# Regrouping the small f32 products of a two-block transformer kernel on one Trainium2 core

## The chip, the cores and the metric

The kernel runs on one core of one Trainium2 chip. The metric is the device time of one execution in microseconds (us), from which the median of the runs is taken. On the chip, TensorE does matrix products in program order; its instructions appear under PE (the product) and PEld (the load of its stationary operand). VectorE (DVE), ScalarE (ACT) and GpSimd (POOL) do the rest, and SyncE (SP) and POOL issue transfers.

## The reference

Two blocks of two layers each over 256 tokens of width 1024, all in f32. The first block's even layer mixes tokens with differential attention and with HGRN2, its odd layer with dilated attention; each layer has a squared-relu FFN. The second block carries 256 latents and 256 context tokens; each layer mixes with gated linear attention (4 heads of 64), neighbourhood attention and sliding-window attention, and has a SwiGLU. Where the change lies, this is computed:

```python
def hgrn2(hq, hf, hi, hg, lb, out_g):            # 4 heads, keys and values of 128, chunks of 64
    ...
    a = jnp.einsum('nbhtk,nbhsk->nbhts', qc * jnp.exp(b - b_mid), kc * jnp.exp(b_mid - b))
    a = jnp.where(jnp.tril(jnp.ones((C, C), bool)), a, 0.0)
    o_intra = jnp.einsum('nbhts,nbhsv->nbhtv', a, vc)
    ...
    def step(state, xs):
        qo, ks, vv, dc = xs
        o_inter = jnp.einsum('bhtk,bhkv->bhtv', qo, state)
        state = dc[..., None] * state + jnp.einsum('bhsk,bhsv->bhkv', ks, vv)
        return state, o_inter

def gla_chunked(q, k, v, log_a, s0):             # 4 heads of 64, chunks of 64, both directions
    ...
    a_intra = jnp.where(lower, jnp.einsum('bhncd,bhnsd->bhncs', q_in, k_in), 0.0)
    o_intra = jnp.einsum('bhncs,bhnse->bhnce', a_intra, vc)
    chunk_state = jnp.einsum('bhnsd,bhnse->bhnde', k_end, vc)
    ...
    o_inter = jnp.einsum('bhncd,nbhde->bhnce', q_in, s_enter)
    o = (o_intra + o_inter).reshape(B, H, T, dv).astype(v.dtype)
    return o, s_final
```

## The kernel before

A token tile is 128 tokens, so each stream has two (t = 0, 1), and a token tile holds two chunks of 64 (c = 0, 1). Weights stream from HBM and are split into a high and a low part (`wh`, `wl`; L214 on ScalarE, L216 on VectorE); a projection is three products each (L279 to L281 in the first block and in projections in general, L325 to L327, L826 to L828 and L851 to L853 in the FFN, L1465 to L1467, L1544 to L1546 and L1570 to L1572 in the second block's SwiGLU). Products of attention and of the recurrences are plain f32; transposes (L177) go through TensorE too.

The program is a list of items (a projection's block, a step of attention, a row of the modulation), woven by hand. Their instructions are then put in order on each engine by a scheduler that simulates times, so a change in one item can move others. PSUM has eight banks under four tags: `acc` 4, `sc` 2, `sm` 1, `fil` 1. A product that needs a bank waits until the earlier tile of that tag has been read.

The places that matter:
- `hg2` (L620 to L637): HGRN2's output of a token tile. For each chunk and head an intra-chunk product of 64x64 (L620, `aT` holds the masked scores, zero between the chunks), for chunks after the first also one with the state (L622); then per chunk the four state products (L627), which VectorE turns into the next state (L630, L633). ScalarE copies the result (L637). The out-projection (L279) follows.
- `sums` in `gla` (L1091): for each chunk four products of 64 rows give the chunk's state sums, copied by VectorE into `gcs` (L1094, L1095).
- `scores` in `gla` (L1113): for each chunk four products of 64 rows give the scores, masked by VectorE (L1116).
- `outputs` in `gla` (L1154): for each chunk and head two intra-chunk products (one per direction; contraction over 128 tokens, 64 of them zero, 64 output rows), then up to two with the states entering the chunk.
- `one` in `attention` (L1220): for each of a pair's two heads, the scores against its own keys and, in the latents, against the context's.

The modulation (L955) multiplies weights that POOL loads into two buffers (`fr`, L953); its items are woven among the others. In `gla` and `attention` the class `Stream` chooses PSUM tags: the latents (`ctx` false) use `acc` and `sc`, the context `fil` and `sm`.

Of the kernel before, what the change touches and what calls it, by code (L numbers as in the profile page):

```python
# [14 lines left out]
ALU = mybir.AluOpType  # L15
AX = mybir.AxisListType

P = 128
# [10 lines left out]
def unit_plan():  # L29
    """[k block, k blocks, columns, their number] of the pieces in which each weight is loaded."""  # L30
# [89 lines left out]
def body(ctx: ExitStack, tc: tile.TileContext, A: dict, out: bass.AP):  # L120
# [62 lines left out]
    def params():  # L183
        """feature-major gains of the second block and conditioning vectors."""
# [51 lines left out]
    def weave(a, b, ahead=False):  # L236
        """items of b spread evenly between those of a."""
# [72 lines left out]
    def projT(w, kdim, c0, nb, xs, evac, tag="acc"):  # L310
        """items of a projection to feature-major: nb blocks of 128 columns, two to a tile of evac(tiles)."""
# [24 lines left out]
    class Rot:  # L336
        """PSUM tiles from several tags in turn."""
# [10 lines left out]
    def urgent(fn, offset=URG):  # L348
        """fn, whose instructions go ahead of others that are ready."""
        def f(*args):  # L350
            with tc.high_priority(offset=offset):
                return fn(*args)
        return f

    def split_evac(hi, lo, ps):
        """psum -> hi/lo f32r."""
        S.copy(hi, ps)
        V.tensor_tensor(lo, ps, hi, ALU.subtract)

    def to_xT(src, xT, t, ps_of, g=None, b=None):  # L360
        """token-major [128, 1024] -> feature-major hi/lo, optional per-feature scale/shift."""
# [26 lines left out]
    def ln_half(t, ci, st):  # L388
        """statistics of one finished half of token tile t."""
# [4 lines left out]
    def layer_norm(t, st, l, n, xT):  # L394
        """token tile t normalised with gain and shift in place, and its transpose."""
# [18 lines left out]
    def rms_rstd(ms, tag, eps=1e-6):  # L414
        """1 / rms from the mean squares of the halves."""
# [3 lines left out]
    def head_rms(ps, nh, hd, eps, tag):  # L419
        """psum [P, nh, hd] -> rstd [P, nh]."""  # L420
# [7 lines left out]
    def masked(ps3, d):  # L428
        """select the in-chunk causal positions of [P, 4, P] scores; zero elsewhere."""
# [5 lines left out]
    # ---------------------------------------------------------------------- block 1  # L435

    class XT:
        """a transposed array: high and low parts of its token tiles, and of both tiles side by side."""
# [19 lines left out]
    def rope1(tl, t, nh):  # L458
        """partial rope in place on token-major tl [P, nh, 64]."""
# [11 lines left out]
    def qkT_evac(ps, dst, t, scale, n):  # L471
        """rope and transpose n columns of q or k; dst [P, n / 128, 256]."""
# [10 lines left out]
    def softmax_pair(ps, mask, nk):  # L483
        """ps: two score tiles [P, nk]; returns unnormalised p [P, 2, nk] and 1 / sums [P, 2]."""
# [12 lines left out]
    def pipeline(steps, *stages):  # L497
        """items: the first stage of step i goes with the second of step i - 1 and so on."""
# [9 lines left out]
    # -------- even mixer  # L508
    def even_mixer(xs, y, ynew):
# [4 lines left out]
        def setup():  # L514
# [16 lines left out]
            # lower bounds: softmax over the two rows, four heads on four partitions, then to all of them  # L531
# [32 lines left out]
        def hg1a(t):  # L564
            """cumulative decays of one token tile, feature-major, and to the end of the chunk."""
# [45 lines left out]
        def hg2(t):  # L611
            qo, kst, dec, aT = hgq[t]
            vv = st["vv"]
            o3 = q4(PT("acc"))
            for c in range(2):
                n = 2 * t + c
                r = slice(64 * c, 64 * c + 64)
# [1103 lines left out]
```

## Time and profile before

| | |
|---|---|
| runs | 1965.17, 1967.50, 1971.89 us; median 1967.5 us |
| profiled execution, span from first to last instruction | 1978.5 us; no other time of it was taken |
| that span against the median | 11.0 us longer |
| mean granted TensorE clock | 0.968 |
| PE busy | 1894.7 us, 96% |
| VectorE, ScalarE, GpSimd busy | 1233.7 us, 1006.1 us, 169.4 us |
| transfers | 338.89 MB, mean 171 GB/s |

The profile is of one execution. Busy shares say which engine holds the kernel on the whole; which wait ends last in a stage has to be read from that stage. An f32 product shows up as two matmul instructions, a transpose as one. "us" of a group in the timeline includes the time in which its last product runs out, so durations of a stretch are better read from start to start.

### The profile page before, as it was taken

What the parts mean: (1) busy time and instruction counts of PE and PEld (TensorE: products, weight loads), DVE (VectorE), ACT (ScalarE), POOL (GpSimd) and SP (SyncE); (2) the same over time, 40 slices, a digit from 0 to 9 for tenths busy, and PEclk for the clock granted to TensorE, in tenths of its full rate; (3) what the DMA queues carried; (4) which work ended last, traced back from release to release, by engine and by line L of the source; (5) the groups of instructions that cost most, each with busy time, mean ns of one, the idle gap of its engine ahead of it and who ended that gap; (6) DMA issues with size and microseconds to landing.
All of it is one profiled execution on the core that took longest, in us unless ns stands there. A gap on an engine that the chain in (4) does not pass through costs nothing. (4 is left out here: it accounts for less than half of the span.)

```text
span 1978.5 us, 32280 instructions
## 1 busy us (share of the span) xinstructions
PE 1894.7 (96%) x12593; PEld 1605.1 (81%) x12593; DVE 1233.7 (62%) x2325; ACT 1006.1 (51%) x1669; POOL 169.4 (9%) x230
## 2 busy tenths in 40 slices
PE   8989999997999889999999999999999999989998
PEld 6766798887688578887687988999999996669997
DVE  5563656647467466765767775577655667754455
ACT  6353555535456355554556663354546556344443
POOL 3111300003100030000300000000000000210000
PEclk9997999999899879999999999999999999989999
DMA  8753654544576545456553345555665455455663
GB/s 288 244 168 127 233 188 152 179 139 150 187 223 210 173 148 172 141 165 216 177 167 116 99 141 169 158 181 180 183 184 160 136 180 168 140 170 167 183 184 107
DMA packets 101540, 338.89 MB, mean 171 GB/s; under 512 B 12212, under 2 KB 13516, under 8 KB 101388
## 3 DMA queue, kind: packets, MB, share of 16 engines
q1 hardware_dynamic: 86124, 286.00, 46.0%
q0 software_dynamic: 15264, 50.84, 7.7%
q8 instruction: 99, 1.62, 0.3%
q14 instruction: 53, 0.43, 0.1%
HBM read 335.73 MB, written 1.05 MB: 170 GB/s over the span
## 5 line engine op out<-in xcount | busy, mean ns | idle before, releaser
L216 DVE TENSOR_TENSOR wl<-wr,wh 128x1024 fp32r<-128x1024 f32 (+3 forms) x562 | 646.3, 1153 | 408.4 <-ACT wh L214 399.2
L214 ACT CAST wh<-wr 128x1024 fp32r<-128x1024 f32 (+3 forms) x562 | 549.1, 980 | 623.8 <-PE sc L1466 123.3
L279 PE MATMUL acc<-wh,mh 128*128 128x256 f32 (+3 forms) x400 | 131.4, 336 | 2.7 <-ACT mh L378 2.0
L280 PE MATMUL acc<-wl,mh 128*128 128x256 f32 (+3 forms) x400 | 131.2, 329 | 2.4 <-DVE wl L216 2.4
L281 PE MATMUL acc<-wh,ml 128*128 128x256 f32 (+3 forms) x400 | 131.0, 330 | 0.0
L279 PE MATMUL acc<-wh,xh 128*128 128x512 f32 (+3 forms) x304 | 120.0, 401 | 4.1 <-ACT wh L214 2.2
L280 PE MATMUL acc<-wl,xh 128*128 128x512 f32 (+3 forms) x304 | 118.8, 392 | 0.2
L281 PE MATMUL acc<-wh,xl 128*128 128x512 f32 (+3 forms) x304 | 117.3, 387 | 0.1
L953 POOL DMA_DIRECT2D fr<-in_w_mod_dram x90 | 48.9, 545 | 646.8 <-PE fil L955 532.9
L851 PE MATMUL acc<-wh,a 128*128 128x512 f32 x256 | 101.4, 400 | 0.0
L852 PE MATMUL acc<-wl,a 128*128 128x512 f32 x256 | 101.0, 395 | 0.0
L853 PE MATMUL acc<-wh,a 128*128 128x512 f32 x256 | 100.9, 396 | 0.0
L1465 PE MATMUL sc<-xh,wh 128*128 128x256 f32 x352 | 100.8, 286 | 0.0
L1466 PE MATMUL sc<-xl,wh 128*128 128x256 f32 x352 | 100.2, 285 | 0.0
L1467 PE MATMUL sc<-xh,wl 128*128 128x256 f32 x352 | 100.1, 285 | 0.0
L1466 PE MATMUL sc<-ml,wh 128*128 128x256 f32 x352 | 98.9, 281 | 0.0
L1465 PE MATMUL sc<-mh,wh 128*128 128x256 f32 x352 | 98.8, 281 | 0.0
L1467 PE MATMUL sc<-mh,wl 128*128 128x256 f32 x352 | 98.7, 280 | 0.0
L955 PE MATMUL fil<-fr,cT 128*32 128x256 f32 x720 | 64.9, 427 | 25.9 <-DMA fr<-in_w_mod_dram 25.8
L279 PEld LDWEIGHTS acc<-wh,mh 128*128 128x128 f32 x400 | 75.1, 189 | 15.5 <-issue 4.8
L280 PEld LDWEIGHTS acc<-wl,mh 128*128 128x128 f32 x400 | 75.7, 189 | 9.1 <-DVE wl L216 3.1
L281 PEld LDWEIGHTS acc<-wh,ml 128*128 128x128 f32 x400 | 75.4, 189 | 7.3 <-issue 0.6
(574 smaller groups left out, 4912.6 us busy)
## 6 DMA issues: line engine op xcount, KB each, us to landing
wr<-in_ffn_w_dram SPq DMA_DIRECT2D x128, 512.0 KB, 3.5
fr<-in_w_mod_dram POOLq DMA_DIRECT2D x90, 512.0 KB, 4.8
wr<-in_w_gate_dram SPq DMA_DIRECT2D x66, 512.0 KB, 3.8
wr<-in_w_up_dram SPq DMA_DIRECT2D x66, 512.0 KB, 4.2
wr<-in_w_down_dram SPq DMA_DIRECT2D x66, 512.0 KB, 3.8
wr<-in_w_in_dram SPq DMA_DIRECT2D x40, 384.0 KB, 3.5
wr<-in_ev_w_in_dram SPq DMA_DIRECT2D x28, 512.0 KB, 5.2
wr<-in_w_in_dram SPq DMA_DIRECT2D x28, 512.0 KB, 3.5
```

The lines of the kernel that those rows point to most:

```text
L214: S.copy(hi, raw)
L216: V.tensor_tensor(lo, raw, hi, ALU.subtract)
L279: mm(o, xh[:, k, :], wh[:, kk, :], start=(u == 0 and kk == 0), stop=False)
L280: mm(o, xh[:, k, :], wl[:, kk, :], start=False, stop=False)
L281: mm(o, xl[:, k, :], wh[:, kk, :], start=False, stop=(u == nu - 1 and kk == 1))
L851: mm(o, hh[:, b, ts_], wh[:, kk, :], start=(b == 0), stop=False)
L852: mm(o, hh[:, b, ts_], wl[:, kk, :], start=False, stop=False)
L853: mm(o, hl[:, b, ts_], wh[:, kk, :], start=False, stop=(b == 3))
L955: mm(ps[32 * g:32 * g + 32, 0:256], cT[:, k, :], raw[:, 256 * g:256 * g + 256], start=(k == 0), stop=(k == KD - 1), tile_position=(0, 32 * g))
L1465: mm(o, wh[:, kk, bs], mh, start=(k == 0 and b == 0), stop=False, skip_group_check=True)
L1466: mm(o, wh[:, kk, bs], ml, start=False, stop=False, skip_group_check=True)
L1467: mm(o, wl[:, kk, bs], mh, start=False, stop=(k == 7), skip_group_check=True)
```

## The change

Five regroupings, and no other work: comments and docstrings that go with them are left out here, and line numbers shift by up to 15.
- `one`: the products of a pair's heads alternate.
- `hg2`: one 128x128 product per head gives the intra-chunk part of both chunks; then the state products of both chunks, head by head; last the products with the states.
- `sums` and `scores`: the products of the two chunks alternate, into two PSUM tiles. The new `e.pair` gives them: `fil` and `acc` in the context (`sm` and `fil` in its last layer, where it has no outputs), `acc` twice in the latents.
- `outputs`: the intra-chunk products over all 128 output rows, eight in place of sixteen, then the products with the states by direction, head and chunk.

```diff
 def hg2(t):
             o3 = q4(PT("acc"))
-            for c in range(2):
-                n = 2 * t + c
-                r = slice(64 * c, 64 * c + 64)
-                for h in range(4):
-                    hs = slice(h * P, (h + 1) * P)
-                    mm(o3[r, h, :], aT[r, h, r], vv[r, t, hs], start=True, stop=(n == 0))
-                    if n > 0:
-                        mm(o3[r, h, :], qo[:, h, r], states[n][:, h, :], start=False, stop=True)
-                if n < 3:
-                    c3 = q4(rot())
+            for h in range(4):
+                mm(o3[:, h, :], aT[:, h, :], vv[:, t, h * P:(h + 1) * P], start=(h == 0), stop=False, skip_group_check=True)
+            ns_ = [n for n in (2 * t, 2 * t + 1) if n < 3]
+            c3s = [q4(rot()) for _ in ns_]
+            for h in range(4):
+                for n, c3 in zip(ns_, c3s):
+                    r = slice(64 * (n % 2), 64 * (n % 2) + 64)
+                    mm(c3[:, h, :], kst[r, h * P:(h + 1) * P], vv[r, t, h * P:(h + 1) * P], start=True, stop=True)
...
+            for h in range(4):
+                for c in range(2):
+                    r = slice(64 * c, 64 * c + 64)
+                    if 2 * t + c:
+                        mm(o3[r, h, :], qo[:, h, r], states[2 * t + c][:, h, :], start=False, stop=(h == 3),
+                           skip_group_check=True)
...
 class Stream:
+            self.pair = (Rot("fil"), Rot("acc")) if self.ctx else (Rot("acc"), Rot("acc"))
...
 def sums(t):
-            for c in range(2):
-                r = slice(64 * c, 64 * c + 64)
-                cs = rot().rearrange("p (d h n) -> p d h n", d=2, h=2)
-                for d in range(2):
-                    for hp in range(2):
-                        mm(cs[:, d, hp, :], ke[r, d, hp * P:(hp + 1) * P], e.v[r, t, hp * P:(hp + 1) * P],
+            cs2 = [new().rearrange("p (d h n) -> p d h n", d=2, h=2) for new in (e.pair if need_out else (Rot("sm"), Rot("fil")))]
+            for d in range(2):
+                for hp in range(2):
+                    for c in range(2):
+                        r = slice(64 * c, 64 * c + 64)
+                        mm(cs2[c][:, d, hp, :], ke[r, d, hp * P:(hp + 1) * P], e.v[r, t, hp * P:(hp + 1) * P],
                            start=True, stop=True)
...
 def scores(t):
-                pa = rot().rearrange("p (d h n) -> p d h n", d=2, h=2)
-                for d in range(2):
-                    for hp in range(2):
-                        mm(pa[:, d, hp, :], en[r, d, hp, :], ep[r, d, hp, :], start=True, stop=True)
+            pa2 = [new().rearrange("p (d h n) -> p d h n", d=2, h=2) for new in e.pair]
+            for d in range(2):
+                for hp in range(2):
+                    for c in range(2):
+                        r = slice(64 * c, 64 * c + 64)
+                        mm(pa2[c][:, d, hp, :], en[r, d, hp, :], ep[r, d, hp, :], start=True, stop=True)
...
 def outputs(t):
-            for c in range(2):
-                r = slice(64 * c, 64 * c + 64)
+            for h in range(4):
+                for d in range(2):
+                    mm(op[h % 2][:, h // 2, :], aT_[t][h % 2][:, d, h // 2, :], e.v[:, t, h * 64:(h + 1) * 64],
+                       start=(h < 2 and d == 0), stop=False, skip_group_check=True)
+            for d in range(2):
                 for h in range(4):
                     hr = slice(64 * (h % 2), 64 * (h % 2) + 64)
-                    vs = e.v[:, t, h * 64:(h + 1) * 64]
-                    ops = [(aT_[t][h % 2][:, d, h // 2, r], vs) for d in range(2)]
-                    for d in range(2):
+                    for c in range(2):
+                        r = slice(64 * c, 64 * c + 64)
                         s0 = states[d, 2 * t + c]
                         if s0 is not None:
-                            ops.append((ep[hr, d, h // 2, r], s0[hr, h // 2, :]))
-                    for i, (a, b) in enumerate(ops):
-                        mm(op[h % 2][r, h // 2, :], a, b, start=(i == 0), stop=(i == len(ops) - 1))
+                            mm(op[h % 2][r, h // 2, :], ep[hr, d, h // 2, r], s0[hr, h // 2, :], start=False,
+                               stop=(d == 1 and h > 1), skip_group_check=True)
...
 def one(hp, t):
-                p = PT(e.sc[c])
-                for i, kk in enumerate(ks):
-                    mm(p[:, i * 256:(i + 1) * 256], q, kk, start=True, stop=True)
-                ps.append(p)
+                ps.append(PT(e.sc[c]))
+                qks.append([(q, kk) for kk in ks])
+            for i, pair in enumerate(zip(*qks)):
+                for p, qk in zip(ps, pair):
+                    mm(p[:, i * 256:(i + 1) * 256], *qk, start=True, stop=True)
```

The scheduler's order on PE shows what this becomes. A row is a line, an operation, its output and inputs (with buffer numbers) and the output's shape; "x4" means four alike in a row. First, `outputs` of the latents in the second block's first layer, before: `a` is the values, `t_2229` and `t_2231` the masked scores, `cf` and `gs` states.

```order
L1154 MATMUL acc_11799<-a_2090_10256,t_2229_10966 64x64 x2
L1154 MATMUL acc_11799<-cf_669_3327,t_2192_10747 64x64
L1154 MATMUL acc_11799<-gs_11633,t_2192_10747 64x64
L1154 MATMUL acc_11800<-a_2090_10256,t_2231_10974 64x64 x2
L1154 MATMUL acc_11800<-cf_669_3327,t_2192_10747 64x64
L1154 MATMUL acc_11800<-gs_11633,t_2192_10747 64x64
```

And after, the same place:

```order
L1152 MATMUL acc_11775<-a_2090_10232,t_2230_10947 128x64 x2
L1152 MATMUL acc_11776<-a_2090_10232,t_2231_10950 128x64 x2
L1152 MATMUL acc_11775<-a_2090_10232,t_2230_10947 128x64 x2
L1152 MATMUL acc_11776<-a_2090_10232,t_2231_10950 128x64 x2
L1161 MATMUL acc_11775<-cf_669_3319,t_2192_10723 64x64
L1161 MATMUL acc_11775<-gs_11594,t_2192_10723 64x64
L1161 MATMUL acc_11776<-cf_669_3319,t_2192_10723 64x64
L1161 MATMUL acc_11776<-gs_11594,t_2192_10723 64x64
```

Before, the two kinds of product take turns for 32 products; after, eight products of the one kind come first and then 16 of the other, with nothing between.

Second, the end of `hg2` up to the out-projection, before (L622 with L620 in turn goes on to the end, with L697, L177, L955 and four L627 between):

```order
L955 MATMUL fil_1179<-fr_1243,cT_72 32x256 x4
L622 MATMUL acc_1267<-t_302_1277,t_97_438 64x128
L620 MATMUL acc_1267<-a_264_1130,t_123_565 64x128
L622 MATMUL acc_1267<-t_302_1277,t_97_438 64x128
L620 MATMUL acc_1267<-a_264_1130,t_123_565 64x128
```

After, from the same modulation group on:

```order
L958 MATMUL fil_1179<-fr_1243,cT_72 32x256 x4
L177 MATMUL sm_1229<-ident_61,t_274_1162 128x128 x2
L637 MATMUL acc_1267<-t_303_1282,t_97_438 64x128 x4
L637 MATMUL acc_1325<-t_304_1284,t_136_612 64x128
L700 MATMUL acc_1350<-a_194_870,a_259_1107 128x128 x6
L958 MATMUL fil_1179<-fr_1313,cT_72 32x256 x4
L177 MATMUL sm_1233<-ident_61,t_289_1216 128x128 x2
L623 MATMUL sm_1330<-a_264_1130,t_137_613 128x128 x4
L700 MATMUL acc_1350<-a_194_870,a_259_1107 128x128 x2
L958 MATMUL fil_1179<-fr_1319,cT_72 32x256 x4
L637 MATMUL acc_1325<-t_313_1335,t_136_612 64x128
L637 MATMUL acc_1325<-t_304_1284,t_136_612 64x128
```

The products with the states (L637) stand in runs, the intra-chunk ones have left this stretch for an earlier place, and a modulation group (`fr_1443`) now stands between the last L637 and the out-projection's first L279.

Third, the context's `sums` of its first token tile among the first block's FFN, before (the second chunk's four follow 28 rows later in the same way):

```order
L826 MATMUL sc_2722<-xh_1619,wh_2643 128x256
L1091 MATMUL fil_2699<-c_430_1947,t_559_2693 128x128 x4
L827 MATMUL sc_2722<-xl_1620,wh_2643 128x256
```

After:

```order
L829 MATMUL sc_2714<-xh_1611,wh_2635 128x256
L1095 MATMUL fil_2691<-c_430_1939,t_559_2685 128x128
L1095 MATMUL acc_2692<-c_430_1939,t_559_2685 128x128
L1095 MATMUL fil_2691<-c_430_1939,t_559_2685 128x128
L1095 MATMUL acc_2692<-c_430_1939,t_559_2685 128x128
```

Both chunks' products (eight in all) now stand together and alternate between two PSUM tiles.

## Rows read from the trace of the kernel before

**Rows 1.** The page, busy us (share of the span) and instructions of each engine.
```profile
PE 1894.7 (96%) x12593; PEld 1605.1 (81%) x12593; DVE 1233.7 (62%) x2325; ACT 1006.1 (51%) x1669; POOL 169.4 (9%) x230
```
**Rows 2.** Waits of PE: line, releaser, us in total, times, longest.
```profile
PE fil L955 <- DMA fr<-in_w_mod_dram: 25.8, 17, 4.8
PE fil L177 <- DVE t L1348: 10.2, 1, 10.2
PE sc L826 <- ACT mh L378: 7.0, 1, 7.0
```
**Rows 3.** Two stretches: busy us of each engine, granted clock, DMA share, GB/s.
```profile
core 0: us, PE busy (x) PEld busy (x) DVE busy (x) ACT busy (x) POOL busy (x), PEclk, DMA share, GB/s
146.00:170.00 24.00, 23.81 (x97) 12.85 (x96) 4.06 (x14) 0.73 (x2) 1.58 (x3) 0.50 0.31 97
1690.00:1735.00 45.00, 43.09 (x428) 31.45 (x426) 29.53 (x111) 18.53 (x54) 9.58 (x16) 1.00 0.40 129
```
**Rows 4.** Timeline of PE, `outputs` of the latents: start us, us, instructions.
```profile
1200.25 0.45 PE L1154 MATMUL acc<-a,t 128*64 128x64 f32 x4
1200.63 0.33 PE L1154 MATMUL acc<-cf,t 64*64 64x64 f32 x2
1200.79 0.28 PE L1154 MATMUL acc<-gs,t 64*64 64x64 f32 x2
...
1206.23 0.39 PE L1544 MATMUL fil<-xh,wh 128*128 128x256 f32 x1
```
**Rows 5.** The same for the context's first token tile.
```profile
406.12 0.45 PE L1154 MATMUL acc<-c,t 128*64 128x64 f32 x4
...
411.63 0.39 PE L826 MATMUL sc<-xh,wh 128*128 128x256 f32 x1
```
**Rows 6.** Timeline of PE, runs of narrow full-size tiles and of 64-column tiles.
```profile
308.01 1.05 PE L1067 MATMUL fil<-cst,t 128*128 128x128 f32 x8
308.82 0.36 PE L826 MATMUL sc<-xh,wh 128*128 128x256 f32 x1
...
1113.20 0.66 PE L1277 MATMUL acc<-fr,sv 128*64 128x128 f32 x8
1113.69 0.61 PE L1277 MATMUL acc<-fr,csv 128*64 128x128 f32 x8
```
**Rows 7.** PE in the context's `sums`: groups of L1091, then the timeline around one.
```profile
L1091 PE MATMUL fil<-c,t 64*128 64x128 f32 x32 | 4.6, 285 | 0.0
...
317.31 0.28 PE L826 MATMUL sc<-xh,wh 128*128 128x256 f32 x1
317.51 1.16 PE L1091 MATMUL fil<-c,t 64*128 64x128 f32 x8
318.60 0.39 PE L827 MATMUL sc<-xl,wh 128*128 128x256 f32 x1
318.82 0.28 PE L828 MATMUL sc<-xh,wl 128*128 128x256 f32 x1
```
**Rows 8.** Timeline of PE, attention's score products of one pair of heads.
```profile
1023.01 0.71 PE L1220 MATMUL sc<-a,a 64*128 64x256 f32 x4
...
1024.08 0.39 PE L279 MATMUL acc<-wh,xh 128*128 128x256 f32 x1
```
**Rows 9.** Timeline of PE, the latents' `scores`, both chunks in a row.
```profile
1125.49 1.71 PE L1113 MATMUL acc<-t,t 64*128 64x128 f32 x16
1127.13 0.50 PE L1570 MATMUL acc<-wh,c 128*128 128x512 f32 x1
```
**Rows 10.** Timeline of PE, HGRN2: idle time before and its releaser in brackets.
```profile
144.31 0.64 PE L955 MATMUL fil<-fr,cT 128*32 128x256 f32 x8 [1.43 <-DMA fr<-in_w_mod_dram]
146.79 0.69 PE L622 MATMUL acc<-t,t 128*64 128x128 f32 x2
147.41 0.69 PE L620 MATMUL acc<-a,t 64*64 64x128 f32 x2
...
170.49 0.79 PE L279 MATMUL acc<-wh,mh 128*128 128x512 f32 x1 [0.68 <-ACT t L637]
```

More of the change, by code (lines that the diff above doesn't have):

```diff
@@ L614, in hg2 @@
             o3 = q4(PT("acc"))
-            for c in range(2):
-                n = 2 * t + c
-                r = slice(64 * c, 64 * c + 64)
-                for h in range(4):
-                    hs = slice(h * P, (h + 1) * P)
-                    mm(o3[r, h, :], aT[r, h, r], vv[r, t, hs], start=True, stop=(n == 0))
-                    if n > 0:
-                        mm(o3[r, h, :], qo[:, h, r], states[n][:, h, :], start=False, stop=True)
-                if n < 3:
-                    c3 = q4(rot())
-                    for h in range(4):
-                        hs = slice(h * P, (h + 1) * P)
-                        mm(c3[:, h, :], kst[r, hs], vv[r, t, hs], start=True, stop=True)
-                    ns = t2([P, 4, P])
-                    if n == 0:
-                        V.tensor_copy(ns, c3)
-                    else:
-                        for h in range(4):
-                            V.scalar_tensor_tensor(ns[:, h, :], states[n][:, h, :], dec[:, h, c:c + 1], c3[:, h, :],
-                                                   ALU.mult, ALU.add)
-                    states[n + 1] = ns
+            for h in range(4):
+                mm(o3[:, h, :], aT[:, h, :], vv[:, t, h * P:(h + 1) * P], start=(h == 0), stop=False, skip_group_check=True)
@@ new lines, in hg2 @@
+            ns_ = [n for n in (2 * t, 2 * t + 1) if n < 3]
[4 more added lines that the diff above has]
+                    mm(c3[:, h, :], kst[r, h * P:(h + 1) * P], vv[r, t, h * P:(h + 1) * P], start=True, stop=True)
+            for n, c3 in zip(ns_, c3s):
+                ns = t2([P, 4, P])
+                if n == 0:
+                    V.tensor_copy(ns, c3)
+                else:
+                    for h in range(4):
+                        V.scalar_tensor_tensor(ns[:, h, :], states[n][:, h, :], dec[:, h, n % 2:n % 2 + 1], c3[:, h, :],
+                                               ALU.mult, ALU.add)
+                states[n + 1] = ns
@@ L1085, in sums @@
             dec_[t] = dec
-            for c in range(2):
-                r = slice(64 * c, 64 * c + 64)
-                cs = rot().rearrange("p (d h n) -> p d h n", d=2, h=2)
-                for d in range(2):
-                    for hp in range(2):
-                        mm(cs[:, d, hp, :], ke[r, d, hp * P:(hp + 1) * P], e.v[r, t, hp * P:(hp + 1) * P],
+            cs2 = [new().rearrange("p (d h n) -> p d h n", d=2, h=2) for new in (e.pair if need_out else (Rot("sm"), Rot("fil")))]
[4 more added lines that the diff above has]
+                        mm(cs2[c][:, d, hp, :], ke[r, d, hp * P:(hp + 1) * P], e.v[r, t, hp * P:(hp + 1) * P],
                            start=True, stop=True)
+            for c, cs in enumerate(cs2):
                 cc = T([P, 2, 2, 64], F32, "gcs", 4)
@@ L1107, in scores @@
             aT_[t] = []
-            for c in range(2):
-                r = slice(64 * c, 64 * c + 64)
-                pa = rot().rearrange("p (d h n) -> p d h n", d=2, h=2)
-                for d in range(2):
-                    for hp in range(2):
-                        mm(pa[:, d, hp, :], en[r, d, hp, :], ep[r, d, hp, :], start=True, stop=True)
+            pa2 = [new().rearrange("p (d h n) -> p d h n", d=2, h=2) for new in e.pair]
[4 more added lines that the diff above has]
+                        mm(pa2[c][:, d, hp, :], en[r, d, hp, :], ep[r, d, hp, :], start=True, stop=True)
+            for pa in pa2:
                 a = t2([P, 2, 2, P])
@@ L1207, in one @@
                     nc.sync.dma_start(nbt[0], A["na_bias"][l, hp])
-            ps = []
+            ps, qks = [], []
             mx = T([P, 2, 2], F32, e.p + "mx2", 3)
```

2 lines of the change are left out of this document (removed).

## The prediction
> **What bounds the kernel now.** I read the busy shares first, then the waits of PE (TensorE's matmuls), then single stretches of PE's timeline where the changed products run. PE is busy for 96% of the span [rows 1]; all its idle time is some 84 us, of which the largest single causes are the modulation weights (25.8 us in 17 waits), one wait of 10.2 us for a normalisation and one of 7.0 us [rows 2]. So nearly everywhere a microsecond less of work on PE is a microsecond less of span, as long as the next thing in PE's queue is ready. In the HGRN2 stage this can be seen directly: between 146 and 170 us PE is busy for 23.81 of 24 us, VectorE for 4.06 and ScalarE for 0.73, and TensorE's granted clock is 0.50, the 1.2 GHz level [rows 3]. No transfer and no other engine holds PE there; it holds them.
>
> An f32 product stands in the trace as two instructions; I count these and call them records.
>
> **The linear attention's output products (`outputs`).** Before, a token tile of the latents takes 64 records, in turns of four with a 128-row, 64-column weight tile (the intra-chunk products) and four with a 64x64 tile (the products with the state). The tile at 1200 us begins at 1200.25 and the next instruction starts at 1206.23: 5.98 us, and a turn of four comes round every 0.37 us, 0.093 us a record [rows 4]. The context's first tile has 56 records (two of its states are zero): 5.51 us [rows 5]. After, the order shows 16 records of 128x128 in one run and then 32 (context: 24) of 64x64 in one run. Full-size records of narrow products cost 0.81/8 = 0.10 us at 308 us [rows 6]; I take 0.11, as the shape in front is another one: 1.8 us. The state records are not to be seen in one run before. Upper bound: the 0.093 us of today without the switch of shape that comes every four; a turn at 1200.63 with two records in 0.16 us gives 0.08 each even so [rows 4], and I put the bound at 0.06. Lower bound: neighbouring records now write different column halves, and 64-column records in that arrangement, twice as wide, come every 0.49/8 = 0.06 us [rows 6], so half of it, 0.03. That is 0.9 to 1.9 us, of which I take 0.9, since the rows at 1113 us are such alternating tiles; the two switches that are left I estimate at 0.3 us. Sum 3.0 us (to 4.0). Saved: 3.0 us in each of four latent tiles (2.0 to 3.4), 12 us; in each of the two context tiles 5.5 - (1.8 + 0.7 + 0.6) = 2.4 us (1.9 to 2.8), 4.8 us. Together **16.8 us** (12 to 19). The merged product itself saves almost nothing: 16 records at 0.11 stand for 32 at 0.06. What goes is the switching every four records.
>
> The Trainium skill speaks against the merging: "TensorEngine Tiling (Array Packing)", in its overview and in "When to Use Tiling", wants a contraction of 64 or less kept as two row tiles, for up to twice the speed, which a merged 128x128 product gives up. By it the intra-chunk part would be better off split and regrouped. The rows at 1200 us show today's 64-wide tiles coming four to 0.37 us; whether split tiles in another order would overlap, no run here shows yet, and the rule alone would take the 12 us to the lower bound of 8.
>
> **The state products of the context (`sums`).** Eight clusters of four products with one 64-row tile (in the first layer 32 records [rows 7], in the second as many) run alone. At 317 us the instruction before starts at 317.31, the cluster at 317.51 and the second instruction behind at 318.82; two plain instructions are 0.12 us each, so the cluster costs 1.51 - 0.24 = 1.27 us [rows 7], of which 8 records at 0.11 are 0.9 and the change of shape 0.4. After, both chunks alternate between two row halves and two PSUM banks, in four clusters of 16. For alternating rows the score products of attention are the nearest row: 16 records of 256 columns between 1023.01 and 1024.08, 0.067 us each [rows 8]. At 0.06 the double cluster costs 1.0 + 0.4 = 1.4 in place of 2.5. Saved 4 x 1.2 = **4.8 us** (1.6 if only the switch is saved, 5.6 at best).
>
> **The same in the latents (`sums`, `scores`).** There both chunks already run back to back, 16 records in 1125.49 to 1127.13, 1.64 us [rows 9]; alternated, 1.4 at most and 1.1 at least: 0.4 us in each of eight clusters, **3.5 us** (0 to 4.5). The context's score clusters stay split by the scheduler in the order after; I cost them at nothing.
>
> **HGRN2 (`hg2`).** In the half-clock stretch L622 and L620 take turns, 128x64 and 64x64, a pair of records every 0.62 us [rows 10]. Ten L620 pairs and all twelve L622 pairs (24 records) lie there. The order after has all intra-chunk products (L617) ahead, at full clock, where they cost 16 x 0.11 = 1.8 us against the 1.3 of the six early L620 pairs (12 records at the same 0.11); so 10 x 0.62 = 6.2 us go and 0.5 come. The L622 pairs (L637 after) come in runs of 4, 1 and 7: 24 records at 0.12 to 0.21 us of half clock plus three switches of 0.3 are 3.8 to 5.9 us in place of 12 x 0.62 = 7.4. Against that: the third state product now follows right behind a transpose into the one `sm` buffer and waits for VectorE's copy of it, some 0.7 us, as does the 0.7 us wait of L279 now [rows 10]; and one more modulation group of about 1 us is moved ahead of the out-projection. Its data are no wait: its buffer comes free some 5 us before. The out-projection should start at 163 to 164 instead of 170.49: **7 us** (3 to 10; if the clock does not fall at all, the remaining 17 us of half-clock work shrink by half and it is 15).
>
> **Attention's score products.** Whole groups (both heads, 16 records) already overlap: 1.07 us [rows 8]. The alternation as such is worth nothing. But the scheduler left 36 contiguous runs of them in the latents and now leaves 28; a run less is a switch of 0.4 us less: 3 us, of which I take **2** (0 to 3), since some gaps were beside other row products.
>
> **Sum.** 16.8 + 4.8 + 3.5 + 7 + 2 = 34 us of PE time. Not all reaches the end. Modulation weights are re-issued when PE has freed their buffer, so part of what is saved ahead of such a wait is waited out: 17 waits with a mean of 1.5 us [rows 2], of which some four lie behind the changed places; in the second latent layer (1690 to 1735 us) PE is idle for 1.9 us already and VectorE is busy for two thirds of the time [rows 3], so that there PE will wait for the masks and normalisations. I take off 5 us (0 to 12). Net -29 us: the profiled span of 1978.5 would be 1949.5. The profiled execution is 11 us above the median of the runs; the change is absolute and I carry it over: 1967.5 - 29 = **1938.5 us**. VectorE, ScalarE, GpSimd and SP keep their instructions in number; the order moves some of them, under PE's cover.
>
> **Rivals.**
> 1. The regrouping only removes switches: state records stay at 0.06 us and row halves do not overlap better than today. Then outputs 12, context sums 1.6, HGRN2 6, scores 2, less 3: 18 us, 1949 us. For it: nothing before shows 64x64 tiles in a favourable order. Against: [rows 6] and [rows 8] show both kinds of overlap. Chance 0.2. The rule above on split tiles would end here too.
> 2. Waits eat it: PE reaches each wait for weights, masks and normalisations earlier and stands there; the 12 us of the bound and half of the rest are lost, about 12 us are left, 1955 us. Against: 96% busy [rows 1]. Chance 0.12.
> 3. The clock stays high through HGRN2: another 8 to 10 us, about 1929 us and, with the upper bounds, down to 1922. For it: the low clock comes with just these small products [rows 3, 10]. Against: before 146 us PE also stood idle for 1.43 us on a weight transfer, and that stays. Chance 0.1.
> 4. Slower: the dense overlapped clusters, with the idle time behind them, bring TensorE to the 1.2 GHz level in the latents' stages, as the stage at 146 us has it. There the low level lasts 27 us, of which half is lost, 13.5 us; in four such stages it is 54 us, less the 34 saved: 1988 us. It decides if three of the four stages fall. Against: 1690 to 1735 us is full of such products and stands at 1.00 [rows 3]. Chance 0.04.
> 5. Nothing measurable: rivals 1 and 2 together, or the context's new use of the four `acc` buffers, which the FFN's down products also take, holds PE for 1 to 2 us at each of its eight clusters. The order leaves some 30 matmuls between, which is 4 us, so I expect no wait. Chance 0.04.
>
> **How the numbers follow.** The main case has 0.5 (1931 to 1946 us). A measurement of this kernel can tell about 0.3%, 6 us. Faster by more than that: the main case and rivals 1 to 3, 0.92, less a little for what no row shows: 0.89. Within 0.3%: 0.06. Slower: 0.05. The range takes in the main case, rivals 1 and 2 and most of 3: 1924 to 1957 us.
>
> **What would show it.** Output clusters of the latents at 3 us and of the context at 3.1; L1095 (now L1091) clusters of 16 records in 1.0 to 1.1 us; L279 of the out-projection near 163.5 us and the clock back at 1.00 by 167; PE's busy time down by 30 to 34 us, its waits up by under 5. I am wrong if output clusters last 4 us or more, if the waits of PE grow by over 10 us, or if new stretches at 0.50 appear.

## The result and the profile after

The changed kernel takes 1952.76 us (median of 9 runs, 1948.19 to 1961.66); the kernel before, in runs beside it, 1969.11 us (9 runs). The two medians are 16 us apart; the ratio on record is 0.9898, 95% interval 0.987 to 0.9925, which is some 20 us (15 to 26), where 29 were forecast. The time lies in the range, 14 us above the predicted 1938.5 and above the main case (1931 to 1946 us).

The profiled execution has a span of 1949.5 us, 29.0 less than the one before, which is the forecast of the profiled span to the digit. That is in part luck, as the runs of before showed later: 68 of its executions have spans of 1972.0 us in the mean, and the one that was profiled, 1978.5, lies in the upper fifth of them. The page after:

```profile
span 1949.5 us, 32053 instructions
PE 1859.0 (95%) x12481; PEld 1582.9 (81%) x12481; DVE 1230.2 (63%) x2325; ACT 1006.3 (52%) x1669; POOL 168.0 (9%) x230
```

PE is busy for 35.7 us less than before [rows 1], and idle for 90.5 us in place of 83.8. Both profiles stand at the 1.2 GHz level for about as long, 128 us before and 131 after, but not at the same places: outside HGRN2's stage it is 100 us before and 131 after. The waits of PE after, which answer to [rows 2]:

```profile
PE fil L958 <- DMA fr<-in_w_mod_dram: 30.7, 19, 7.5
PE sc L829 <- ACT mh L378: 9.3, 1, 9.3
PE fil L177 <- DVE t L1357: 8.8, 2, 7.4
```

The modulation weights are waited for 4.9 us longer, the longest wait is 7.5 us in place of 4.8, and the wait of the first block's second FFN has grown by 2.3 us.

**The output products.** Timeline of PE, the latents' `outputs` of layer 0 (L1152 the merged products, L1161 those with the states), against [rows 4]:

```profile
1176.39 1.90 PE L1152 MATMUL acc<-a,t 128*128 128x64 f32 x16
1178.21 0.27 PE L1161 MATMUL acc<-cf,t 64*64 64x64 f32 x1
1178.22 0.27 PE L1161 MATMUL acc<-gs,t 64*64 64x64 f32 x1
1178.23 0.27 PE L1161 MATMUL acc<-cf,t 64*64 64x64 f32 x1
1178.23 0.27 PE L1161 MATMUL acc<-gs,t 64*64 64x64 f32 x1
1178.32 0.22 PE L1161 MATMUL acc<-cf,t 64*64 64x64 f32 x1
...
1178.84 0.38 PE L1553 MATMUL fil<-xh,wh 128*128 128x256 f32 x1
```

2.45 us from start to start, where it was 5.98. Sixteen merged records take 1.82 us, 0.114 each. The 32 records with the states take 0.63 us, 0.02 each: four of them start within 0.02 us of each other, by the program's order one for each quarter of the array, and the next four follow 0.06 to 0.11 us after these. The three other latent tiles take 2.45, 2.55 and 3.26 us, the two context tiles 2.44 each. Before it was 5.92 to 5.97 us four times and 5.51 twice, so 19.3 us went.

**The state products.** The context's `sums` of the first tile, against [rows 7]:

```profile
303.51 0.28 PE L829 MATMUL sc<-xh,wh 128*128 128x256 f32 x1
303.72 0.37 PE L1095 MATMUL fil<-c,t 64*128 64x128 f32 x1
303.72 0.37 PE L1095 MATMUL acc<-c,t 64*128 64x128 f32 x1
303.93 0.27 PE L1095 MATMUL fil<-c,t 64*128 64x128 f32 x1
303.94 0.27 PE L1095 MATMUL acc<-c,t 64*128 64x128 f32 x1
...
304.81 0.39 PE L830 MATMUL sc<-xl,wh 128*128 128x256 f32 x1
```

Sixteen records in 1.09 us, as long as eight took before: the two row halves run as pairs, 0 to 10 ns apart.

**HGRN2.** The out-projection's first L279 starts at 153.74 us in place of 170.49 [rows 10]:

```profile
141.40 0.64 PE L958 MATMUL fil<-fr,cT 128*32 128x256 f32 x8 [1.54 <-DMA fr<-in_w_mod_dram]
144.55 1.09 PE L637 MATMUL acc<-t,t 128*64 128x128 f32 x10
151.83 1.09 PE L637 MATMUL acc<-t,t 128*64 128x128 f32 x14
153.74 0.50 PE L279 MATMUL acc<-wh,mh 128*128 128x512 f32 x1
```

Between 139 and 154 us the granted clock is 1.00. In this execution it is rival 3: the stage was not only shorter, it was not at the 1.2 GHz level at all.

### The profile page after: what moved, and what is told of

Same layout as the page of the kernel before. It is cut to its first block, busy times and chain, and to the rows that moved or that the text cites. A ratio compares the mean times of both kernels' runs of the same rounds, so it can differ in the third digit from the quotient of the medians.

```text
span 1949.5 us, 32053 instructions
## 1 busy us (share of the span) xinstructions
PE 1859.0 (95%) x12481; PEld 1582.9 (81%) x12481; DVE 1230.2 (63%) x2325; ACT 1006.3 (52%) x1669; POOL 168.0 (9%) x230
## 5 line engine op out<-in xcount | busy, mean ns | idle before, releaser
L279 PE MATMUL acc<-wh,mh 128*128 128x256 f32 (+3 forms) x400 | 131.8, 336 | 0.0
L279 PE MATMUL acc<-wh,xh 128*128 128x512 f32 (+3 forms) x304 | 119.9, 401 | 2.6 <-ACT xh L378 1.9
L1474 PE MATMUL sc<-mh,wh 128*128 128x256 f32 x352 | 98.7, 280 | 0.0
L958 PE MATMUL fil<-fr,cT 128*32 128x256 f32 x720 | 65.9, 422 | 31.2 <-DMA fr<-in_w_mod_dram 30.7
L279 PEld LDWEIGHTS acc<-wh,mh 128*128 128x128 f32 x400 | 75.2, 189 | 12.4 <-issue 4.8
L829 PE MATMUL sc<-mh,wh 128*128 128x256 f32 x256 | 74.1, 291 | 9.3 <-ACT mh L378 9.3
```

The lines of the kernel that those rows point to most:

```text
L279: mm(o, xh[:, k, :], wh[:, kk, :], start=(u == 0 and kk == 0), stop=False)
L829: mm(o, wh[:, kk, bs], mh, start=(k == 0 and b % 2 == 0), stop=False, skip_group_check=True)
L1474: mm(o, wh[:, kk, bs], mh, start=(k == 0 and b == 0), stop=False, skip_group_check=True)
```

## The experiments

Each execution comes with its span and its mean granted clock. From these I work out two numbers. The time at the 1.2 GHz level is 2 x (1 - mean clock) x span. The clock-free span is the span less half of that time; it is a measure, not a time that was run. For the 68 executions of before the first number goes from 86 to 139 us, and the span grows by 0.42 us for each of these us (correlation 0.95), so most of the scatter of this kernel goes with the clock; as 0.42 is less than a half, the measure takes off a little too much. The clock-free span scatters by 1 to 3 us only. Each kernel ran beside the kernel before, in one of several batches, and a ratio compares within the batch. The mean of before at the lower level is 110 to 115 us in the four batches that show it.

| kernel | ratio to before, 95% | mean us at the 1.2 GHz level | clock-free span, us |
|---|---|---|---|
| before, 68 executions | 1 | 113 | 1915.7 |
| before, unchanged, as a run of its own | 1.001 (0.9984 to 1.0036) | 116 | 1915.8 |
| the change, 9 and 6 runs | 0.9898 (0.987 to 0.9925), 0.989 (0.9858 to 0.9921) | 125 | 1889.4 |
| outputs alone | 0.9881 (0.985 to 0.9913) | 103 | 1897.2 |
| HGRN2 alone | 0.9956 (0.9933 to 0.9979) | 102 | 1914.3 |
| sums and scores alone | 0.9957 (0.9927 to 0.9986) | 122 | 1902.0 |
| attention's scores alone | 1.0033 (1.0002 to 1.0063) | 125 | 1917.1 |
| the change without HGRN2's part | 0.9895 (0.9857 to 0.9934) | 129 | 1888.3 |
| the change without attention's part | 0.9837 (0.9805 to 0.9869) | 107 | 1885.5 |
| the change, old product order in attention | 0.9854 (0.9815 to 0.9893) | 114 | 1884.4 |
| the change, outputs split by columns | 0.9874 (0.9844 to 0.9904) | 130 | 1883.1 |
| the same without attention's part | 0.9811 (0.9785 to 0.9837) | 110 | 1879.2 |
| outputs split, sums and scores | 0.9845 (0.9808 to 0.9883) | 120 | 1881.3 |

**1. Before once more.** The kernel is unchanged.

> The kernel before, unchanged, profiled a second time. Theory A: the granted clock of 0.50 from 146 to 173 us comes from this kernel's HGRN2 products; the second profile shows it again, with the out-projection's first L279 near 170.5 us. Theory B: which stretches fall to the lower level differs from one execution to the next; then HGRN2 may stand at 1.00 here, L279 comes near 160 us, and the span is some 10 us under 1978.5. Time: the same as before, ratio 1.000 within 0.4%.

HGRN2 fell again, but for less long: 17 us, with L279 at 166.55. Kernels further down that have the same HGRN2 code differ as much. One window of each trace, by its granted clock (the column before the last two): before again; outputs alone, whose `hg2` is the old one; the change without HGRN2's part; attention's scores alone.

```profile
143.50:161.00 17.50, 17.50 (x77) 9.68 (x71) 2.94 (x10) 0.59 (x1) 1.05 (x2) 0.51 0.28 90
```
```profile
140.00:158.00 18.00, 16.82 (x121) 10.28 (x122) 7.18 (x23) 2.64 (x10) 2.11 (x4) 1.00 0.61 212
```
```profile
144.50:175.50 31.00, 30.32 (x114) 17.74 (x113) 6.63 (x20) 6.91 (x29) 3.78 (x6) 0.50 0.27 84
```
```profile
144.00:175.00 31.00, 30.32 (x116) 17.93 (x116) 6.21 (x19) 6.16 (x25) 3.71 (x6) 0.50 0.27 84
```

In seven profiles the old `hg2` stands at the lower level for 17 to 31 us (five times), for 3 us or not at all. Theory B holds, though not in this one profile: the same code falls in one execution and not in another. In the seven profiles with the new `hg2` the stretch is 0 to 10 us long.

**2. Outputs alone.**

```diff
# before, with outputs() of the change and nothing else
+            for h in range(4):
+                for d in range(2):
+                    mm(op[h % 2][:, h // 2, :], aT_[t][h % 2][:, d, h // 2, :], ...
```

> Only the linear attention's outputs are regrouped (eight 128x128 products, then the products with the states). Theory A (terms add up): six clusters of 2.45 to 2.6 us in place of four of 5.97 and two of 5.5, 19 us less of PE time, and 14 to 19 us less of time, ratio 0.990 to 0.993. Rival (waits eat it): clusters as short, but PE waits grow by 8 us or more, ratio 0.995 to 0.998.

1950.0 us, ratio 0.9881, more than forecast and as fast as the whole change. Clock-free it is 18.5 us less, which is what went from the clusters in this profile (34.8 us before, 16.3 here); the rest is less time at the lower level. The rival falls: PE is idle for 81.3 us in place of 83.8, so nothing of it is waited out.

**3. HGRN2 alone.**

```diff
# before, with hg2() of the change and nothing else
+                mm(o3[:, h, :], aT[:, h, :], vv[:, t, h * P:(h + 1) * P], start=(h == 0), ...
```

> Only HGRN2's output is regrouped. Theory A: the regrouped products keep the 2.4 GHz level through the stage, the out-projection's L279 starts near 154 us instead of 170.5, and 10 to 13 us of the 17 stay to the end: ratio 0.9935 to 0.995. Theory B: the clock level is drawn anew in each execution and the regrouping as such is worth 6 to 8 us: ratio 0.996 to 0.997, and L279 somewhere between 154 and 164 us as the clock falls.

Ratio 0.9956, some 9 us, but clock-free only 1.4 us; the rest is the lower level (102 us in place of 113). L279 starts at 159.26 us, with 10 us at 0.50 in the stage. Theory B, in the main: clock-free the regrouped products are 2.5 us ahead at the out-projection, and 0.4 us at 271 us (times in before), so most of it is waited out behind the stage. In the mean of 12 runs the gain is there all the same (the interval lies below 1), and most of it is the lower level; in company it does not show, as experiment 6 has it.

**4. Sums and scores alone.**

```diff
# before, with e.pair, sums() and scores() of the change
+                    for c in range(2):
+                        mm(cs2[c][:, d, hp, :], ke[r, d, hp * P:(hp + 1) * P], ...
```

> Only sums and scores of the linear attention alternate their chunks between two PSUM tiles. Theory A: four clusters of 16 records of 1.09 us in the context's sums in place of eight of 1.08, and 1.1 in place of 1.5 to 1.64 in the latents: 5 + 4 = 9 us less of PE time, 6 to 9 us less of time, ratio 0.9955 to 0.997. Rival: the context's products in the acc tiles hold the FFN's accumulators up, PE waits grow by as much, ratio 0.999 to 1.002.

Ratio 0.9957, as expected; clock-free 13.7 us less, more than the 9 of the clusters, with 9 us more at the lower level against it. Of the other 5 us, 3.3 can be found: the latents' attention scores, whose code is here as before, stand in 32 contiguous runs of 35.5 us in all, where before has 37 of 38.9 us. The scheduler, with the new order in front of it, breaks up fewer of them. The last 2 us stay open. The waits for the `acc` banks that rival 5 named do not appear (PE is idle for 84.7 us in place of 83.8).

**5. Attention's score products alone.**

```diff
-                p = PT(e.sc[c])
-                for i, kk in enumerate(ks):
-                    mm(p[:, i * 256:(i + 1) * 256], q, kk, start=True, stop=True)
+            for i, pair in enumerate(zip(*qks)):
+                for p, qk in zip(ps, pair):
+                    mm(p[:, i * 256:(i + 1) * 256], *qk, start=True, stop=True)
```

> Only the score products of a pair's heads alternate. I compare the span less half of the time at the 1.2 GHz level (clock-free span), 1915.7 us before. Theory A: the alternation itself is worth nothing, but the scheduler leaves the groups whole more often, and a half group takes 1.06 us as a whole one does: clock-free span 4 to 8 us less, ratio 0.996 to 0.999 with the clock level drawn at random. Rival: it is this part that makes the sum of the parts (-33.6 us clock-free for the other three alone) larger than the whole (-27.2): clock-free span 4 to 8 us more.

Slower by 0.33%, interval just above 1. The latents' score products themselves did get shorter, summed over the timeline 36.0 us in 28 contiguous runs in place of 38.9 in 37; the clock-free span is 1.4 us longer all the same, and the time at the lower level 12 us. So neither came: not the 4 to 8 us less of theory A, and not the rival's 4 to 8 us more.

**6. The change again, and without one part.** `after_again` is the change unchanged; `no_hg2` has the old `hg2`, `no_one` the old score products; `tiles_first` takes both PSUM tiles first, as the change does, and then does the products in the old order:

```diff
-            for i, pair in enumerate(zip(*qks)):
-                for p, qk in zip(ps, pair):
+            for p, head in zip(ps, qks):
+                for i, qk in enumerate(head):
                     mm(p[:, i * 256:(i + 1) * 256], *qk, start=True, stop=True)
```

> The changed kernel, unchanged, once more beside the others. Theory A: clock-free span 1888.5 within 3 us, and some 127 us at the lower clock level, more than the 114 of before, so that the time is 18 to 22 us less: ratio 0.988 to 0.9915. Theory B: the lower level's total was drawn high in the nine runs; it comes back to 114 us and the ratio to 0.986.

> The changed kernel with HGRN2's output as before. Theory A: HGRN2's regrouping is worth 1.4 us clock-free, as alone: clock-free span 1889 to 1892, the time within 5 us of the changed kernel's. Theory B: HGRN2's regrouping sets the order downstream and costs there what the parts lose against their sum: clock-free span 1882 to 1886 and the time 4 us or more below the changed kernel's.

> The changed kernel with attention's score products as before (one head after the other). Theory A: alternating them makes PE wait for the second bank and moves waits to places where the clock then falls (as at 1599 us); without it the clock-free span is 1 to 3 us under the changed kernel's 1889.4, the time at the lower level is some 10 us shorter, and the time 4 to 8 us less: ratio 0.9855 to 0.9875. Rival: the alternation saves in the combination what it does not save alone; clock-free span 2 us or more above, ratio 0.990 or more.

> The changed kernel, with both PSUM tiles of a pair taken before the score products as in the change, but the products in the old order, one head after the other. Theory A (the alternating order of the products is what costs): PE's order is then that of the kernel without the regrouping of attention, so ratio 0.982 to 0.9855, some 107 us at the lower level and no wait of 7 us at the modulation weights. Rival (taking both tiles early is what costs): as the changed kernel, ratio 0.988 to 0.991.

The change repeats: 0.989, 122 us at the lower level, so that level was not drawn high in the first nine runs. Without HGRN2's part it is the same kernel in time (0.9895), so its 9 us alone are not found again in company. Without attention's part it is at 0.9837, faster than forecast and 10 to 12 us faster than the change; in `tiles_first` it is at 0.9854. PE's order is the same in these two kernels, instruction by instruction, and clock-free they are 4 and 5 us below the change: the alternating order of the products is what costs, not the early banks. In time alone the interval of `tiles_first` still touches the change's. Of the 10 to 12 us, 4 are clock-free; half of the 18 us less at the lower level would be 9, but some 4 of the 18 can belong to the batches, which were not the same.

Where the 4 are lost is seen on the way through the program. The table gives how far each kernel is ahead of before, clock-free, at the same projection products of both traces (profiled executions; the left column is the time in before). Two profiles of one kernel differ by 1 to 4 us in it, as the two columns of the change show.

| at us | outputs alone | sums, scores alone | attention alone | the change | the change again | without attention | split, without attention |
|---|---|---|---|---|---|---|---|
| 271 | -1.0 | -0.9 | -0.2 | 1.9 | 1.3 | 1.6 | 1.2 |
| 570 | 7.1 | 3.2 | 0.7 | 14.1 | 13.3 | 13.4 | 13.7 |
| 1260 | 13.8 | 5.6 | 1.0 | 24.5 | 22.4 | 21.5 | 25.0 |
| 1613 | 13.7 | 10.2 | 1.0 | 29.0 | 27.0 | 26.0 | 29.6 |
| 1738 | 20.5 | 11.6 | -0.2 | 34.1 | 29.7 | 33.3 | 37.1 |
| 1808 | 19.7 | 12.3 | -0.1 | 30.7 | 26.6 | 32.7 | 37.1 |

Up to 1613 us the change is ahead of the kernel without attention's part; from there to 1808 it gains 1.7 us (in its second profile it loses 0.4) and the other 6.7. Two places in that stage stand out. The first, among the scores of layer 1, in the change:

```profile
1596.69 0.70 PE L1230 MATMUL sc<-a,a 64*128 64x256 f32 x2
1597.23 0.59 PE L1230 MATMUL sc<-ck,a 64*128 64x256 f32 x2
1599.15 1.66 PE L1230 MATMUL sc<-a,a 64*128 64x256 f32 x3 [1.33 <-DVE mx L1243]
1600.16 1.06 PE L1230 MATMUL sc<-ck,a 64*128 64x256 f32 x2
1602.03 1.11 PE L177 MATMUL sm<-ident,t 128*128 128x128 f32 x4
1605.61 0.50 PE L279 MATMUL acc<-wh,mh 128*128 128x512 f32 x1
```

and in the kernel without attention's part:

```profile
1593.38 0.71 PE L1228 MATMUL sc<-a,a 64*128 64x256 f32 x4
1593.92 0.60 PE L1228 MATMUL sc<-ck,a 64*128 64x256 f32 x4
1595.92 0.65 PE L177 MATMUL sm<-ident,t 128*128 128x128 f32 x4 [1.39 <-DVE t L1256]
1597.96 0.50 PE L279 MATMUL acc<-wh,mh 128*128 128x512 f32 x1
```

Both wait some 1.4 us for VectorE. The old order waits once the pair's scores are done; the change waits ahead of the next pair's, whose banks VectorE still reads, and then has the whole pair in front of the transposes and the projection. And there the clock falls: 0.69 in the mean of 1595 to 1606 us against 1.00 in the other kernel's 1593 to 1604. A fall of 3 to 7 us at this place is in all five profiles with alternating scores (the change twice, alone, without HGRN2's part, with the split) and in none of the nine without them, which all wait 1.4 us ahead of the transposes. Of the 21 us that the change's profile stands longer at the lower level than that of the kernel without attention's part, 7 are here.

The second is the end of the stage, where the modulation weights are waited for, in the change and in the kernel without attention's part:

```profile
1726.60 1.07 PE L958 MATMUL fil<-fr,cT 128*32 128x256 f32 x16
1735.22 1.08 PE L958 MATMUL fil<-fr,cT 128*32 128x256 f32 x8 [7.55 <-DMA fr<-in_w_mod_dram]
```
```profile
1719.75 1.07 PE L958 MATMUL fil<-fr,cT 128*32 128x256 f32 x16
1725.90 0.64 PE L958 MATMUL fil<-fr,cT 128*32 128x256 f32 x8 [4.05 <-DMA fr<-in_w_mod_dram]
```

Here the change loses 3.4 us between the last two rows of the table, the other 0.6. In both kernels six groups are left behind the out-projection, and the awaited transfer is issued at the same point, 1.74 us after the last L279 starts; it takes 7.6 us to land in the change and 5.1 in the other. The transfers issued within the same half microsecond, in the change and in the other kernel, with the time to landing in us at the end:

```profile
fr<-in_w_mod_dram POOLq DMA_DIRECT2D x1, 512.0 KB, 7.6
wr<-in_w_up_dram SPq DMA_DIRECT2D x1, 512.0 KB, 7.3
```
```profile
fr<-in_w_mod_dram POOLq DMA_DIRECT2D x1, 512.0 KB, 5.1
```

In the change the SwiGLU's next weights (`wr`, L212) follow 0.16 us behind the modulation's; in the other kernel they follow 1.10 us behind. The four profiles that have alternating scores beside the regrouped outputs, sums and scores all show some 0.16 us and 6.9 to 7.6 us to landing; attention's part alone shows 1.10 us, and there the wait is 4.4 us. So it is the combination. That the two transfers hold each other up is likely, not tested; why the scheduler's order comes out so I can't say.

**7. Outputs split by columns.** Sixteen 128x64 products that alternate between the column halves in place of eight merged ones, once on the whole change, once without attention's part, once without that and HGRN2's.

```diff
                 for d in range(2):
-                    mm(op[h % 2][:, h // 2, :], aT_[t][h % 2][:, d, h // 2, :], e.v[:, t, h * 64:(h + 1) * 64],
+                    for c in range(2):
+                        r = slice(64 * c, 64 * c + 64)
+                        mm(op[h % 2][r, h // 2, :], aT_[t][h % 2][:, d, h // 2, r], e.v[:, t, h * 64:(h + 1) * 64],
```

> The changed kernel, but the intra-chunk products of the linear attention's outputs are not merged: sixteen products of 128x64 that alternate between the two column halves. Theory A (tiles of one shape and different columns overlap, as the state products now do at 0.02 us a record): 32 records in 1.0 us in place of 16 in 1.82, clusters of 1.7 us in place of 2.45, 5 us less in six clusters, ratio 0.986 to 0.988. Rival (the merged product is the better): 32 records at 0.058, clusters of 2.5 us or more, no gain.

> As the one before, and the intra-chunk output products split into column halves that alternate. Theory A: 6 us less clock-free than without the split, as in the changed kernel (1889.4 to 1883.1), so 1880 to 1883, ratio 0.983 to 0.9855. Rival: the split's gain goes into the waits for the modulation weights: within 2 us of the one before.

> Only the parts that pay alone: outputs with split, alternating column halves, and sums and scores alternating; HGRN2 and attention's scores as before. Theory A: the parts add up clock-free, 1915.7 - 18.5 - 5 - 13.7 = 1878.5, and HGRN2's low-clock stretch is there in some executions: ratio 0.982 to 0.9855. Rival (HGRN2's regrouping shortens the low stretch and carries 4 us): 4 us or more slower than the one before.

The split on the whole change, its `outputs` of the latents:

```profile
1182.47 1.15 PE L1154 MATMUL acc<-a,t 128*64 128x64 f32 x32
1183.56 0.27 PE L1163 MATMUL acc<-cf,t 64*64 64x64 f32 x1
...
1184.18 0.39 PE L1555 MATMUL fil<-xh,wh 128*128 128x256 f32 x1
```

Thirty-two records in 1.09 us, 0.034 each, in place of sixteen in 1.82, and a cluster of 1.71 us in place of 2.45. Clock-free it is worth 6.3 us in both places where it was tried; in time the ratios go from 0.989 to 0.9874 and from 0.9837 to 0.9811, with intervals that overlap. Without attention's part it gives the fastest kernel of the study, 1935.97 us against 1972.8 of before, 0.9811 (0.9785 to 0.9837). Leaving HGRN2's part out as well makes 0.9845; the intervals overlap, so the 6 us between them are likely, not shown. They would be the lower level: clock-free the two differ by 2 us.

## Why the prediction was right, and where not

Direction, range and bound were right: PE's work was the limit. The main case did not come: the time lies near the figures of rivals 1 and 2 (1949 and 1955 us), but rival 1's mechanism did not come and rival 2's only in small (PE idle for 6.7 us more), so that it is the width of the range that holds the time. That 35.7 us of PE's work went where 34 were summed is luck as well: the steps as the profiles show them add up to some 44, against which stands the growth of the lower level outside HGRN2's stage, 31 us. The prediction named new stretches at 0.50 as a sign of being wrong, and they appeared. By the steps:

- **Outputs**, 16.8 us predicted, 19.3 measured, 18.5 of them in the clock-free span. The merged records cost 0.114 us as forecast (0.11). The state records were mis-sized: 0.02 us in place of 0.03, as four quarters of the array overlap and not two. That the merged product itself saves nothing was right, and more: split in alternating columns it is 0.7 us shorter a cluster. So the Trainium skill ("TensorEngine Tiling (Array Packing)", "When to Use Tiling") held against the merge, once the products stood in an order that lets the tiles overlap: beside row tiles that section names column tiles, for a left operand of 64 columns, and it is these that ran here, at 1.09 us for what takes 1.82 merged. Row tiles, of which the prediction speaks, were not run for these products. The rows of before could not show any of that, and rival 1, which the rule was tied to, did not come: the state products overlap in any case.
- **Context's sums**, 4.8 predicted; four clusters of 1.09 in place of eight of 1.08 are 4.3. With the switches at both ends, counted as in [rows 7], a double cluster costs 1.28 us and a single one 1.27, so 5.1 us went. The price came from a miscounted row: [rows 8] holds 8 records and not 16, 0.134 us each at 256 columns. Half of it, for half the columns, is 0.067, and 1.09/16 is 0.068, so the number held by its own luck.
- **Latents' sums and scores**, 3.5 predicted. Six of the eight clusters went from 1.4 to 1.64 us down to 0.99 to 1.1, 3 us. The other two were broken up by the scheduler and lay in stretches at the lower level; in this profile they take 4.4 us in place of 2.8, so that 1.4 us are left.
- **HGRN2**, 7 predicted. The profile shows 16.7, the runs 9 us alone and nothing that shows in company, the clock-free measure 1.4 to 3. The step that failed is the price: 0.62 us a pair was read from a stretch at 1.2 GHz as if the kernel always had it. It has it in most executions that were profiled, for 3 to 31 us, and not in all.
- **Attention's scores**, 2 gained predicted; 0.33% lost alone, 10 to 12 us in this combination. The products got 2.8 us shorter alone, so the count of switches was right. But the regrouped sums and scores bring that by themselves (35.5 us without attention's part, 36.2 in the change), so in company nothing was left to gain. What the step left out: an alternating pair needs both banks of `sc` before it gets anywhere, so the whole pair waits for the softmax before it, and this moves the items behind it.
- **Given back**, 5 predicted. Clock-free it was 3.4 us at the modulation weights after 1738 us, and 6 or so in all: the four parts alone add up to 18.5 + 1.4 + 13.7 - 1.4 = 32.2, the whole is 26.3. Not in the sum at all was the clock: 125 us at the lower level in place of 113, half of which is 6 us.

So -26 clock-free and +6 by the clock make the 20 us. Rival 4 named the right effect, new stretches at the lower level in the latents' stages, and gave it 54 us; the whole growth of that level costs about a tenth of that. Its reason, dense clusters with idle time behind them, is not shown: the growth goes with attention's part, as without it the level is 107 us. Rival 3 was right for the profiled execution, but the old `hg2` has such executions too.

## What to carry to other kernels

Price switches of tile shape and the order of tiles, not the count of products: small f32 products of one shape that alternate over row halves, column halves or quarters overlap, those that stand in runs on one tile do not, and a merge into one full-size product is worth less than that. Change one group at a time where a scheduler orders the rest: one part of five, which alone cost 0.33%, cost 10 to 12 us in company. And before a stretch at the lower clock is priced, see a second execution; here one pair of profiles made a part that is worth 9 us in the mean alone, and 1.4 us without the clock, look like 17.

## What the runs showed of the hardware

- Products on the two row halves that alternate start 0 to 10 ns apart, and 16 take what 8 did (1.09 us); on the two column halves 32 records take 1.09 us, 0.034 each; on four quarters 32 records of 64x64x64 take 0.63 us. Before, in turns of four of two shapes, a record came every 0.093 us.
- The clock scatter: one program, unchanged, spent 86 to 139 us of some 1970 at 1.2 GHz, and this accounts for most of the spread of its times, 1961 to 1986 us.
- In 172 of the 185 stretches at the lower level in the 14 profiles PE had stood idle for 1 us or more shortly before, or did so in the stretch; in 13 it had not (0.3 us at 1693.5 us in the second profile of before). A wait of 1.3 us among the attention's score products, of 64 rows, went with a fall in five profiles of five; a wait of 1.4 us ahead of the transposes at the same place went with none in nine. Why the one and not the other is open.
- A transfer of 512 KB with one of another queue issued 0.16 us behind it took 7.6 us to land, and 5.1 us where that one came 1.10 us behind; a third was issued some 0.55 us behind in both.
